# Final norm of a decoder step on one Trainium2 core: the factor table and three residuals are copied to PSUM and read there by VectorE

## The chip, the core and the metric

The kernel runs on one core of a Trainium2 chip. A core has five engines with a queue of instructions each: TensorE (PE in the profile, its weight loads PEld), VectorE (DVE), ScalarE (ACT), GpSimd (POOL) and SyncE (SP), which here only issues transfers. Tensors lie in the on-chip SBUF (128 partitions) or in the smaller PSUM, into which TensorE writes its products; VectorE and ScalarE reach both. The metric is the device time of one execution in microseconds (us), the median over several runs.

## What is computed

The reference is one step of a decoder layer: attention and a gated recurrence, then a mixture of experts, each between two RMS norms. 512 prompt rows and 8 sample rows of 1024 numbers pass through it. The change touches only the last line of the layer:

```
ffn = hier_moe(h, ...)
x = x + gt_f * rms_norm(ffn, g_post_ffn[l])

def rms_norm(x, g):
    y = xf * lax.rsqrt(jnp.mean(xf * xf, axis=-1, keepdims=True) + NORM_EPS)
    return (y * g).astype(x.dtype)
```

In words: each row of the experts' sum is multiplied by a factor per column (gate times norm weight), then by one number per row (the reciprocal root mean square), and the residual `x` is added.

## The kernel before

Everything up to the end of the experts stays as it was. Each expert's last step scatters 96 rows, adding them into the DRAM tensor `Y` (indirect transfer of GpSimd, line 1669). The last of them is issued in `finish(len(units) - 1, ...)`. Ahead of it the residuals are loaded into tiles of the ring of weight buffers, which is free by then: `at_end[t]` for t = 0 to 3 (128 rows each) and 4 (the 8 sample rows), and `GF`, the factors of the prompt's columns repeated on 128 partitions, is loaded into a sixth such tile. All of these are SBUF tiles; in the trace they go by the ring's names (`x`, `ewr`). After a branch that is taken only if an expert overflowed, the pool `fp` is opened and `srow` loads `gfs`, the 8 sample rows' own factors (tile `row`, issued on ScalarE's queue, line 1305).

Then comes the final norm, a loop over t in the order 4, 0, 1, 2, 3:

- SyncE loads 128 rows (8 for t = 4) of `Y` into a tile `y` (line 1837).
- ScalarE squares the row and sums it up into `ssf` (line 1841), and takes the square root (line 147).
- The product with the factors, `yg` (line 1842), is on VectorE for t in `ONDVE` = (0, 3) and on GpSimd for 4, 1 and 2.
- VectorE takes the reciprocal of `ssf` (line 148).
- VectorE's `scalar_tensor_tensor` (line 1846) computes `yg` * `ssf` + residual into `y`; for t = 3 in two halves.
- SyncE writes `y` out (line 1847).

The order of each queue at this place is made by a scheduler, so it isn't quite the order of the code. Each engine takes its own queue in order and waits for what an instruction needs. All elements are 32-bit floats.

Of the kernel before, what the change touches and what calls it, by code (L numbers as in the profile page):

```python
# [11 lines left out]
F32 = mybir.dt.float32  # L12
# [4 lines left out]
AF = mybir.ActivationFunctionType  # L17
ALU = mybir.AluOpType
AX = mybir.AxisListType
PSUM = bass.MemoryType.PSUM  # L20
DRAM = bass.MemoryType.DRAM

D = 1024
# [9 lines left out]
REUSE = "tile"  # L33
# [10 lines left out]
ONDVE = (0, 3)  # L44
# [20 lines left out]
def body(tc, I, O):  # L65
    nc = tc.nc
    es = ExitStack()
    dve, act, pool, pe, sp = nc.vector, nc.scalar, nc.gpsimd, nc.tensor, nc.sync
# [4 lines left out]
    def open_pool(name, bufs, stack, side="left"):  # L73
        return stack.enter_context(tc.tile_pool(name=name, bufs=bufs, side=side, reuse_waits=REUSE))

    psum = []
# [31 lines left out]
    def v2(t):  # L108
        return t.rearrange("p (h n) -> p h n", h=2)
# [35 lines left out]
    def rstd(ss):  # L145

        act.activation(ss, ss, AF.Sqrt, scale=1.0 / D, bias=epst[0:ss.shape[0]])
        dve.reciprocal(ss, ss)  # L148
        return ss
# [1081 lines left out]
    for t in range(5):  # L1231
        n = 128 if t < 4 else 8
# [70 lines left out]
    def srow(pl, g, j, **kw):  # L1303
        row = pl.tile([8, 2, 512], F32, name="row", **kw)
        act.dma_start(row, m4[g, j, :, 0:8, :].rearrange("q r n -> r q n"))
        return row
# [434 lines left out]
    with tc.manual_schedule(engines=MANUAL and {getattr(nc, e).engine for e in MANUAL}):  # L1741
# [5 lines left out]
        for o in ORD_M:  # L1747
            u = k[o] if o in k else 0
            if o in k:
                k[o] += 1  # L1750
                w, c = units[min(u, len(units) - 1)]
# [63 lines left out]
    at_end = [ring[c](F32) for c in ends]  # L1815
    spare = [x for c, x in enumerate(ring) if c not in ends]
    for t in range(5):
        n = 128 if t < 4 else 8
        sp.dma_start(at_end[t][0:n], X1[t, 0:n])
    GF = v2(at_end[5])  # L1820
# [6 lines left out]
    s_w.close()  # L1827


    fp = open_pool("fp", 2, es)  # L1830
    gfs = srow(fp, 1, 1, bufs=1)
    tc.keep_in_program_order(act.preload_act_table_set("sqrt_and_others"))
    ys = []
    for t in (4, 0, 1, 2, 3):
        n = 128 if t < 4 else 8
        y = fp.tile([128, D], F32, name="y", bufs=5)[:n]
        sp.dma_start(y, Y[128 * t:128 * t + n])
        jk = fp.tile([128, D], F32, name="jk")[:n]
        yg = fp.tile([128, D], F32, name="yg", bufs=3)[:n]
        ss = fp.tile([128, 1], F32, name="ssf", bufs=5)[:n]  # L1840
        act.activation(jk, y, AF.Square, accum_out=ss)
        (dve if t in ONDVE else pool).tensor_tensor(v2(yg), v2(y), GF if t < 4 else gfs, op=ALU.mult)  # L1842
        r = rstd(ss)
        out_ = O["yp"][t] if t < 4 else O["ys"]
        for c in (slice(0, 512), slice(512, D)) if t == 3 else (slice(0, D),):
            dve.scalar_tensor_tensor(y[:, c], yg[:, c], r, at_end[t][0:n, c], op0=ALU.mult, op1=ALU.add)  # L1846
            sp.dma_start(out_[:, c], y[:, c])
    es.close()

# [132 lines left out]
```

## Time and profile before

| | |
|---|---|
| median of 3 runs | 790.48 us (789.93 to 792.44) |
| the profiled execution's own time | 791.27 us |
| its span, first to last instruction | 789.6 us |
| busy: TensorE, VectorE, ScalarE, GpSimd | 83%, 59%, 47%, 23% of the span |
| the last `Y` scatter issued by GpSimd | at 761.79 us of the span |
| loads of `y` issued | from 768.35 us |
| last operation of VectorE ends | at 785.67 us |

Busy shares are means over the whole span. The final norm is the last stretch of it, from about 768 us on; TensorE has nothing to do there, and only the instructions of the other four count. Times of the trace are counted from the start of the span, in microseconds; the profiled execution's own time is 1.7 us above its span.

### The profile page before, as it was taken

What the parts mean: (1) busy time and instruction counts of PE and PEld (TensorE: products, weight loads), DVE (VectorE), ACT (ScalarE), POOL (GpSimd) and SP (SyncE); (2) the same over time, 40 slices, a digit from 0 to 9 for tenths busy, and PEclk for the clock granted to TensorE, in tenths of its full rate; (3) what the DMA queues carried; (4) which work ended last, traced back from release to release, by engine and by line L of the source; (5) the groups of instructions that cost most, each with busy time, mean ns of one, the idle gap of its engine ahead of it and who ended that gap; (6) DMA issues with size and microseconds to landing.
All of it is one profiled execution on the core that took longest, in us unless ns stands there. A gap on an engine that the chain in (4) does not pass through costs nothing. (4 is left out here: it accounts for less than half of the span.)

```text
span 789.6 us, 13169 instructions
## 1 busy us (share of the span) xinstructions
PE 651.7 (83%) x4495; PEld 490.3 (62%) x4495; DVE 464.0 (59%) x1140; ACT 374.1 (47%) x759; POOL 183.3 (23%) x208
## 2 busy tenths in 40 slices
PE   3885988998999999897999739995288899999930
PEld 1663866687878788885676426564255577666620
DVE  4523613345867765577643544356865976888806
ACT  4212512334455547623444234445445766888723
POOL 1000310002130131425432112435301223222114
PEclk9898999999999999999999958997588999999975
DMA  8876798866454632106221485338698889998515
GB/s 302 262 256 218 258 315 295 316 197 205 141 175 130 182 118 73 56 4 262 94 81 55 102 303 177 112 123 319 212 358 295 263 222 287 359 333 296 148 29 213
DMA packets 74604, 160.81 MB, mean 204 GB/s; under 512 B 11346, under 2 KB 39538, under 8 KB 74146
## 3 DMA queue, kind: packets, MB, share of 16 engines
q1 hardware_dynamic: 59844, 125.98, 46.6%
q10 hardware_dynamic: 10654, 25.39, 9.9%
q0 software_dynamic: 4032, 8.53, 5.1%
q8 instruction: 37, 0.61, 0.3%
q14 instruction: 37, 0.30, 0.1%
HBM read 145.29 MB, written 24.28 MB: 215 GB/s over the span
## 5 line engine op out<-in xcount | busy, mean ns | idle before, releaser
L563 PE MATMUL pp<-hhi,wh 128*128 128x260 f32 x256 | 75.6, 295 | 0.3 <-ACT kvt L441 0.3
L563 PE MATMUL pp<-hlo,wh 128*128 128x260 f32 x256 | 74.4, 291 | 0.0
L563 PE MATMUL pp<-hhi,wl 128*128 128x260 f32 x256 | 74.2, 290 | 0.0
L1669 POOL DMA_INDIRECT Y<-ot,gi x17 | 24.4, 1438 | 130.1 <-ACT ot L1668 123.0
L563 PEld LDWEIGHTS pp<-hhi,wh 128*128 128x128 f32 x256 | 49.4, 193 | 2.7 <-issue 2.0
L563 PEld LDWEIGHTS pp<-hhi,wl 128*128 128x128 f32 x256 | 49.3, 193 | 2.4 <-issue 2.3
L563 PEld LDWEIGHTS pp<-hlo,wh 128*128 128x128 f32 x256 | 49.4, 193 | 1.4 <-issue 1.2
L655 ACT ACTIVATE jn<-P,M 128x128 bf16<-128x128 f32 (+3 forms) x64 | 35.9, 560 | 27.3 <-DVE M L653 21.8
L113 DVE TENSOR_TENSOR wl<-wr,wh 128x1024 fp32r<-128x1024 f32 x9 | 11.2, 1250 | 39.8 <-ACT wh L112 39.8
L1058 ACT ACTIVATE PT<-mm 128x256 f32<-128x256 f32 x80 | 23.9, 388 | 19.8 <-PE mm L1054 19.7
L1640 PE MATMUL pf<-ewi,xh 128*96 128x512 f32 x72 | 30.2, 419 | 2.0 <-ACT xh L112 2.0
L653 DVE CUSTOM_DVE_ANT_0 P<-mm,tb 128x128 f32<-128x128 f32 (+3 forms) x64 | 29.0, 483 | 4.0 <-PE mm L646 3.9
L397 PE MATMUL mm<-hhi,wh 128*128 128x260 f32 x144 | 29.9, 288 | 1.3 <-ACT wh L112 1.3
L1640 PE MATMUL pf<-ewi,xl 128*96 128x512 f32 x72 | 29.5, 409 | 1.2 <-DVE xl L113 1.2
L112 ACT ACTIVATE wh<-wr 128x1024 fp32r<-128x1024 f32 x9 | 9.5, 1057 | 43.3 <-DMA wr<-in_wi 25.9
L397 PE MATMUL mm<-hlo,wh 128*128 128x260 f32 x144 | 30.0, 285 | 0.0
L397 PE MATMUL mm<-hhi,wl 128*128 128x260 f32 x144 | 29.7, 287 | 0.0
L646 PE MATMUL mm<-ka,qs 128*128 128x512 f32 (+2 forms) x112 | 27.6, 354 | 0.1
L1054 PE MATMUL mm<-qs,ka 128*128 128x512 f32 x80 | 26.6, 405 | 0.0
L1667 ACT ACTIVATE ot<-mm 96x512 f32<-96x512 f32 x17 | 10.1, 594 | 33.3 <-PE mm L1664 33.3
L397 PEld LDWEIGHTS mm<-hhi,wh 128*128 128x128 f32 x144 | 22.2, 188 | 5.0 <-issue 3.4
L299 PEld LDWEIGHTS po<-cg,w1c 128*128 128x128 f32 x160 | 21.5, 214 | 5.7 <-issue 3.3
(651 smaller groups left out, 1885.1 us busy)
## 6 DMA issues: line engine op xcount, KB each, us to landing
ewr<-in_ew SPq DMA_DIRECT2D x37, 512.0 KB
wa<-in_wa SPq DMA_DIRECT2D x16, 1024.0 KB
wr<-in_wi ACTq DMA_DIRECT2D x25, 512.0 KB
ewt<-in_ew SPq DMA_DIRECT2D x24, 512.0 KB
cg<-in_cc SPq DMA_DIRECT2D x64, 128.0 KB
ewh<-in_ew SPq DMA_DIRECT2D x16, 512.0 KB
x<-in_ew SPq DMA_DIRECT2D x15, 512.0 KB
mh<-in_wa SPq DMA_DIRECT2D x13, 512.0 KB
```

The lines of the kernel that those rows point to most:

```text
L113: (eng or dve).tensor_tensor(lo, src, hi.bitcast(F32), op=ALU.subtract)
L299: pe.matmul(p[:, 128 * k:128 * k + 128], w1c[:, k, s, :], cg[:, :, k, s, :], start=(s == 0), stop=(s == 7))
L397: pe.matmul(p[:, hf, 0:260], a[:, k, :], b[:, k, hf * 260:hf * 260 + 260], start=(k == 0 and j == 0), stop=(k == KT - 1 and j == 2))
L563: pe.matmul(p[:, 0:260], a[:, k, :], b[:, k, c], start=(k == 0 and j == 0), stop=(k == KT - 1 and j == 2))
L646: pe.matmul(o, QS[g][:, h % 4, qc], KA[g][:, j, a:b], start=(j == 0), stop=(j == 1))
L653: dve.tensor_tensor_reduce(out=p, in0=sb[:, br], in1=tb0[:, 384 - 128 * i:512].rearrange("p (k n) -> p k n", n=128), scale=SL[h], scalar=1 ...
L655: act.activation(jn[:, 0:128 * (i + 1)], p.rearrange("p k n -> p (k n)"), AF.Exp, scale=-1.0, bias=M[:, 0, i, br, h:h + 1], accum_out=M[:, ...
L1054: pe.matmul(S[:, br], KS[g][:, q, br, j], QS[g][:, :, qc], start=False, stop=(q == 1))
L1058: act.activation(PT[:, :, h], S4[:, :, h], AF.Exp, scale=-SL[4 * g + h])
L1640: pe.matmul(pg, a[:, k, :], b[:, wk_], start=(k == 0 and j == 0), stop=(k == 7 and j == 2))
L1667: act.activation(o3[:, 0], pd[:, 0], AF.Copy)
L1669: pool.indirect_dma_start(out=Y, out_offset=bass.IndirectOffsetOnAxis(ap=gix, axis=0), in_=ot, in_offset=None, bounds_check=T - 1, oob_is_ ...
```

## The change

Two copies of what VectorE reads are put into PSUM before the loop: `GFP`, a copy of `GF` (by VectorE), and `xp0`, `xp1`, `xp4`, copies of the residuals 0 (by VectorE), 1 and 4 (by ScalarE). The PSUM pool of the experts is closed first, and a new one, `fpp`, is opened for the four tiles. VectorE's products of t = 0 and 3 read `GFP`; its `scalar_tensor_tensor` of t = 4, 0 and 1 read the PSUM copies. GpSimd's products still read `GF` in SBUF, and the residuals of t = 2 and 3 stay in SBUF. The loop is cut into three, loads, products and sums, so that all loads are written first; `yg` has 5 buffers instead of 3 and `jk` 1 instead of 2.

```
+    psum.pop(0)[0].close()
+    fpp = es.enter_context(tc.tile_pool(name="fpp", bufs=1, space=PSUM, reuse_waits=REUSE))
     fp = open_pool("fp", 2, es)
+
+    GFP = fpp.tile([128, 2, 512], F32, name="GFP")
+    dve.tensor_copy(GFP, GF)
+    beside = {}
+    for t in (4, 0, 1):
+        n = 128 if t < 4 else 8
+        beside[t] = fpp.tile([128, D], F32, name=f"xp{t}")[0:n]
+        if t:
+            act.activation(beside[t], at_end[t][0:n], AF.Copy)
+        else:
+            dve.tensor_copy(beside[t], at_end[t])
     gfs = srow(fp, 1, 1, bufs=1)
     tc.keep_in_program_order(act.preload_act_table_set("sqrt_and_others"))
     ys = []
+    rows_, r_ = {}, {}
     for t in (4, 0, 1, 2, 3):
         n = 128 if t < 4 else 8
         y = fp.tile([128, D], F32, name="y", bufs=5)[:n]
         sp.dma_start(y, Y[128 * t:128 * t + n])
-        jk = fp.tile([128, D], F32, name="jk")[:n]
-        yg = fp.tile([128, D], F32, name="yg", bufs=3)[:n]
+        rows_[t] = y, fp.tile([128, D], F32, name="yg", bufs=5)[:n]
+    for t in (4, 0, 1, 2, 3):
+        y, yg = rows_[t]
+        n = y.shape[0]
+        jk = fp.tile([128, D], F32, name="jk", bufs=1)[:n]
         ss = fp.tile([128, 1], F32, name="ssf", bufs=5)[:n]
         act.activation(jk, y, AF.Square, accum_out=ss)
-        (dve if t in ONDVE else pool).tensor_tensor(v2(yg), v2(y), GF if t < 4 else gfs, op=ALU.mult)
-        r = rstd(ss)
+        (dve if t in ONDVE else pool).tensor_tensor(v2(yg), v2(y), gfs if t == 4 else GFP if t in ONDVE else GF, op=ALU.mult)
+        r_[t] = rstd(ss)
+    for t in (4, 0, 1, 2, 3):
+        y, yg = rows_[t]
+        n = y.shape[0]
         out_ = O["yp"][t] if t < 4 else O["ys"]
         for c in (slice(0, 512), slice(512, D)) if t == 3 else (slice(0, D),):
-            dve.scalar_tensor_tensor(y[:, c], yg[:, c], r, at_end[t][0:n, c], op0=ALU.mult, op1=ALU.add)
+            dve.scalar_tensor_tensor(y[:, c], yg[:, c], r_[t], beside.get(t, at_end[t][0:n])[:, c], op0=ALU.mult, op1=ALU.add)
             sp.dma_start(out_[:, c], y[:, c])
```

How VectorE's queue changes behind the branch, in one piece of the difference. `x_8103` is `GF`, `ewr_8098` the residual 0, `x_8099` to `x_8102` the residuals 1 to 4; `xp_9627`, `xp_9629`, `xp_9625` are `xp0`, `xp1`, `xp4`:

```order
+L1835 COPY GFP<-x_8103 128x1024
+L1843 COPY xp_9627<-ewr_8098 128x1024
+L1859 TENSOR_TENSOR yg<-y,GFP 128x1024
 L148 RECIPROCAL ssf<-ssf 8x1
-L1842 TENSOR_TENSOR yg<-y,x_8103 128x1024
-L1846 SCALAR_TENSOR_TENSOR y<-yg,ssf,x_8102 8x1024
+L1866 SCALAR_TENSOR_TENSOR y<-yg,ssf,xp_9625 8x1024
 L148 RECIPROCAL ssf<-ssf 128x1
-L1846 SCALAR_TENSOR_TENSOR y<-yg,ssf,ewr_8098 128x1024
+L1866 SCALAR_TENSOR_TENSOR y<-yg,ssf,xp_9627 128x1024
 L148 RECIPROCAL ssf<-ssf 128x1
-L1846 SCALAR_TENSOR_TENSOR y<-yg,ssf,x_8099 128x1024
```

Two copies stand in front; the first product moves ahead of the first reciprocal. Behind these rows the queue goes on with the sum of t = 1, as the next rows show:

```order
+L1866 SCALAR_TENSOR_TENSOR y<-yg,ssf,xp_9629 128x1024
 L148 RECIPROCAL ssf<-ssf 128x1
-L1842 TENSOR_TENSOR yg<-y,x_8103 128x1024
-L1846 SCALAR_TENSOR_TENSOR y<-yg,ssf,x_8100 128x1024
+L1859 TENSOR_TENSOR yg<-y,GFP 128x1024
 L148 RECIPROCAL ssf<-ssf 128x1
-L1846 SCALAR_TENSOR_TENSOR y<-yg,ssf,x_8101 128x512 x2
+L1866 SCALAR_TENSOR_TENSOR y<-yg,ssf,x_8100 128x1024
+L1866 SCALAR_TENSOR_TENSOR y<-yg,ssf,x_8101 128x512 x2
```

The last reciprocal moves ahead of the sum of t = 2. On ScalarE, behind the same branch, the two copies come ahead of the load of `row`:

```order
+L1841 ACTIVATE xp_9625<-x_8102 8x1024
+L1841 ACTIVATE xp_9629<-x_8099 128x1024
 L1305 DMA row<-MOD 8x2x512
-L1832 ACT_TABLE_LOAD
-L1841 ACTIVATE jk,ssf<-y 8x1024
+L1845 ACT_TABLE_LOAD
+L1858 ACTIVATE jk,ssf<-y 8x1024
```

The load of `row` and the loading of the square root's table move back by two copies. GpSimd's three products and SyncE's loads and writes keep their order.

## Rows read from the trace of the kernel before

**Rows 1.** Chain that ended last, first and fifth of its 6 pieces: start, us, what

```profile
781.84 1.12 DVE yg L1842
...
784.26 0.75 DVE y L1846
```

**Rows 2.** Waits of SyncE's queue from 740 us on: us in total, times, longest

```profile
SPq L1837 <- DMA Y<-ewt,gi: 21.7, 1, 21.7
...
SPq L1971 <- DMA out_yp<-y: 1.9, 1, 1.9
```

**Rows 3.** Timeline of VectorE in the final norm: start, duration, instruction [idle before <- releaser]

```profile
772.78 1.22 DVE L1842 TENSOR_TENSOR yg<-y,x 128x1024 f32<-128x1024 f32 x1 [0.81 <-DMA y<-Y]
...
773.92 1.27 DVE L1846 SCALAR_TENSOR_TENSOR y<-yg,ssf,x 8x1024 f32<-8x1024 f32 x1
...
775.12 0.14 DVE L148 RECIPROCAL ssf<-ssf 128x1 f32<-128x1 f32 x1
...
775.30 3.18 DVE L1846 SCALAR_TENSOR_TENSOR y<-yg,ssf,ewr 128x1024 f32<-128x1024 f32 x1
...
778.65 3.11 DVE L1846 SCALAR_TENSOR_TENSOR y<-yg,ssf,x 128x1024 f32<-128x1024 f32 x1
...
781.76 1.20 DVE L1842 TENSOR_TENSOR yg<-y,x 128x1024 f32<-128x1024 f32 x1
...
782.88 1.27 DVE L1846 SCALAR_TENSOR_TENSOR y<-yg,ssf,x 128x1024 f32<-128x1024 f32 x1
...
784.26 1.41 DVE L1846 SCALAR_TENSOR_TENSOR y<-yg,ssf,x 128x512 f32<-128x512 f32 x2
```

**Rows 4.** Timeline of GpSimd: its last scatter and the three products

```profile
761.79 1.40 POOL L1669 DMA_INDIRECT Y<-ewt,gi  x1 [4.72 <-DMA Y<-ot,gi]
...
770.35 2.33 POOL L1842 TENSOR_TENSOR yg<-y,row 8x1024 f32<-8x1024 f32 x1 [7.16 <-DMA y<-Y]
...
774.14 3.27 POOL L1842 TENSOR_TENSOR yg<-y,x 128x1024 f32<-128x1024 f32 x1 [1.45 <-DMA y<-Y]
...
777.36 3.32 POOL L1842 TENSOR_TENSOR yg<-y,x 128x1024 f32<-128x1024 f32 x1
```

**Rows 5.** Timeline near 505 us, VectorE and GpSimd, every input in SBUF

```profile
504.86 2.30 DVE L1377 SCALAR_TENSOR_TENSOR mg<-tg,ssa,tab 128x1024 f32<-128x1024 f32 x1 [0.52 <-POOL tg L1372]
...
504.79 1.28 POOL L1363 TENSOR_TENSOR mg<-x,row 8x512 f32<-8x512 f32 x1
```

**Rows 6.** Timeline near 360 and 390 us; pt and pf are PSUM tiles

```profile
360.42 0.68 DVE L992 TENSOR_TENSOR AT<-pt,triu 128x512 f32<-128x512 f32 x1
...
359.35 2.32 POOL L1102 TENSOR_TENSOR S<-S,hsn 128x1024 f32<-128x1024 f32 x1 [0.53 <-DMA S<-in_s]
...
389.84 1.11 DVE L1000 SCALAR_TENSOR_TENSOR S<-S,sx,pf 128x128 f32<-128x128 f32 x3
...
389.86 0.83 POOL L978 TENSOR_TENSOR qj<-qj,sx 128x384 f32<-128x384 f32 x1
```

**Rows 7.** Groups by line and shape: xcount | busy us, mean ns | idle before

```profile
L1372 POOL TENSOR_TENSOR tg<-x,tab 128x1024 f32<-128x1024 f32 x4 | 9.6, 2390 | 11.6 <-DVE x L1369 7.4 <-issue 2.8 <-DVE ssa L1364 1.4
...
L555 DVE CAST wh<-wr 128x1024 fp32r<-128x1024 f32 x16 | 11.1, 691 | 11.7 <-PE pp L563 7.3 <-DMA wr<-in_wi 3.0 <-PE mm L397 1.4
...
L1000 DVE SCALAR_TENSOR_TENSOR S<-S,sx,pf 128x128 f32<-128x128 f32 x12 | 4.1, 345 | 0.3
```

**Rows 8.** Timeline of ScalarE behind the branch and at its last row

```profile
762.51 0.51 ACTq L1305 DMA_DIRECT2D row<-MOD  x1
763.06 1.28 ACT L1832 ACT_TABLE_LOAD   x1 [3.28 <-ACTq L1824]
...
777.18 1.04 ACT L1841 ACTIVATE jk<-y 128x1024 f32<-128x1024 f32 x1
...
778.35 0.29 ACT L147 ACTIVATE ssf<-ssf,epst 128x1 f32<-128x1 f32 x1
```

**Rows 9.** Windows, one stretch: length; busy PE, PEld, DVE, ACT, POOL; PEclk, DMA share, GB/s

```profile
772.00:774.00 2.00, 0.00 (x0) 0.00 (x0) 1.22 (x2) 1.20 (x3) 0.69 (x1) 0.50 1.03 389
```

## The prediction

> **What bounds the kernel now.** I read the chain of waits first. Its six pieces, from 781.84 us on, lie on VectorE and its queue but for 0.02 us [rows 1], so the final norm's VectorE queue sets the end. SyncE's waits show what stands on either side of it: the loads of `y` wait for the last scatter into `Y`, and at the very end SyncE waits 1.9 us for the last write [rows 2]. The scatter and the write don't change; between them lies the stretch that the change touches.
>
> Then the timeline of VectorE [rows 3]. The reader is to see two durations that don't fit. The sum (`scalar_tensor_tensor`) of 1024 columns takes 1.27 us for t = 4 and for t = 2, but 3.18 for t = 0 and 3.11 for t = 1, same operation, same shape of 1024 columns. Put GpSimd's timeline beside it [rows 4]: its products of 128x1024 take 3.27 and 3.32 us, while four like them elsewhere took 2.39 each [rows 7]. The ends fit a hold in turns. GpSimd's first product starts at 774.14, inside VectorE's sum of t = 4 (773.92 to 775.19); 775.19 + 2.33 = 777.52 against its real end, 774.14 + 3.27 = 777.41. VectorE's sum of t = 0 is issued at 775.30 and ends at 778.48, which is 1.07 behind that end. GpSimd's second product, issued at 777.36, ends at 780.68, 2.20 behind 778.48. VectorE's sum of t = 1 ends at 781.76, 1.08 behind 780.68. So each op waits until the other engine's op is over, then needs about its own length. These four have two tensor inputs in SBUF on both engines. It isn't peculiar to this place: near 505 us a sum of 1024 columns takes 2.30 us, and the GpSimd product beside it ends at 506.07, 1.09 before the sum's end at 507.16 [rows 5].
>
> Does an op with one input in PSUM wait too? Two places answer [rows 6]. A VectorE product of 512 columns with one input in PSUM runs 360.42 to 361.10, wholly inside a GpSimd product (359.35 to 361.67), in 0.68 us. Three sums with exactly the operands that the change makes (tensor in SBUF, a number per row, tensor in PSUM) take 1.11 us together next to a GpSimd product that lies within the same microsecond and takes 0.83; 1.11 / 3 = 0.37, starts and ends overlapping, against a mean of 0.345 over all twelve [rows 7]. Neither is held.
>
> **The change part by part.** *The holds.* The sums of t = 4, 0 and 1, and the product of t = 3, get one input in PSUM, so neither engine should hold the other. I lay VectorE's new queue out with steps from one start to the next, as [rows 3] have them without a hold: product to next 773.92 - 772.78 = 1.14; sum to reciprocal 775.12 - 773.92 = 1.20; reciprocal to next 775.30 - 775.12 = 0.18. The first product starts at 772.78 as now, since it waits for a load. In the new order: product 0 at 772.78; reciprocal 773.92; sum 4 at 774.10; reciprocal 775.30; sum 0 at 775.48; reciprocal 776.68; sum 1 at 776.86; reciprocal 778.06; product 3 at 778.24; reciprocal 779.38; sum 2 at 779.56; the two halves of sum 3 from 780.76, over 1.41 later at 782.17. Now it is 784.26 + 1.41 = 785.67. The gain is 3.50 us. As a check from the other side: the two long sums lose 3.18 - 1.27 = 1.91 and 3.11 - 1.27 = 1.84, together 3.75; the rest is the reciprocal of t = 4, which now stands behind product 0 (it was hidden in a wait), and my cautious step behind it.
>
> *What the new queue waits for.* GpSimd's product 1 starts at 774.14 (a load releases it) and should take 2.39, to 776.53; sum 1 wants it at 776.86. Product 2 then ends at 778.92; sum 2 wants it at 779.56. Both are in time, by 0.33 and 0.64. ScalarE's last root is done at 778.35 + 0.29 = 778.64 [rows 8], and its reciprocal stands at 779.38; of the five it has the least to spare. The last `y` is there by 777.18, when it is squared.
>
> *The copies.* They aren't in the trace. On VectorE two of 128x1024: at least 0.69 (a cast of this size, SBUF to SBUF) [rows 7], at most about a product's 1.22 [rows 3]. I take 1.22, since PSUM is not SBUF and the longer one is the safer; 2.44 in all. The cover is the idle stretch before 772.78: VectorE waits there for `y`, as ScalarE does until the loads come, and what the copies read was loaded before. Without this cover they would cost 1.4 to 2.4. On ScalarE two copies of some 1.05 us each (a square of this size took 1.04, [rows 8]) go ahead of the load of `row`, which moves from 762.51 to about 764.6, and the table from 763.06 to 765.2, over at 766.5. GpSimd needs `row` at 770.35. Loads of `y` issued from about 768.35 on release that instruction within 2.0 us, so a load of the same size issued at 764.6 is there by about 766.6. Cost: nothing.
>
> *PSUM as a source.* From SBUF, a sum of 512 columns takes 0.75 us [rows 1] and one of 1024 takes 1.27 [rows 3]: 0.52 for 512 columns, 0.13 for 128, so 128 columns would be 0.75 - 3 x 0.13 = 0.36. With an input in PSUM they took 0.345 [rows 7]: no dearer; I take zero. At the other end, were the whole 0.37 - 0.345 = 0.03 of [rows 6] its price, five ops would cost 0.13. [...]
>
> *The writes.* Each is 512 KB; at the 389 GB/s of the loads [rows 9] that is 1.35 us, and the sums come at steps of 1.4 to 2.7, so the writes don't pile up more than now. The tail behind the last sum (785.67 to 789.6) stays; I allow 0.4 for it.
>
> Sum: profiled execution 791.27 - 3.50 = 787.8. It stands 0.8 above the median, 790.48, within the runs' spread; from the median, 790.48 - 3.50 = **787.0 us**.
>
> **The rivals.**
>
> *The hold stays.* VectorE still reads `yg` from SBUF in every sum and GpSimd still reads `y` and `GF` there; if the hold comes from any SBUF reading, the change does nothing: 790.5, or 0.2 more for the reciprocal. Against it speak [rows 6], though with ops shorter than these. 8%.
>
> *GpSimd was slow by itself.* If its 3.27 and 3.32 are its own pace here, product 2 ends at 780.68 again; sum 2 starts at 780.7, the halves at 781.9, the end is 783.3: 2.35 gained, 788.1. The 2.39 of [rows 7] speaks against it; that loads run at the same time is for it. 6%.
>
> *The copies hold up the last scatter.* GpSimd prepares it for 1.40 us at 761.79 [rows 4], VectorE is idle then and could be copying. Were GpSimd held for both copies whole, everything behind it, loads included, would come 2.44 later: 790.48 - 3.50 + 2.44 = 789.4; held for part of one, some 788. [...] 5%.
>
> *Slower: reading PSUM is dear at this size.* Five ops on the path (products 0 and 3, sums 4, 0, 1) now read 1024 columns from two PSUM banks; no row has that. At 3.50 / 5 = 0.7 us more for each the gain is gone; slower by over 0.3% it gets from (3.50 + 2.4) / 5 = 1.2 more for each, which is each at twice its length: 792.9 or more. No row of 512 columns shows a trace of it. 4%.
>
> **How the numbers follow.** The forecast has the remaining 77%, and with the bounds above 786.4 to 787.7; runs scattered from 789.93 to 792.44, so that I go down to 785.6 and up to 789.0, which takes in GpSimd's own slowness and a short hold of the scatter. About 0.3%, 2.4 us, is what a measurement of this kernel can tell from no change: faster is below 788.1. Faster: 76 of the 77, half of the 6 and 1 of the 5 make 80%; same: 8 + 3 + 4 + 1 = 16%; slower 4%.
>
> **What the profile after would show.** Right: both VectorE sums of t = 0 and 1 at 1.2 to 1.4 us while GpSimd's products run; those at 2.3 to 2.5 each, with no gap between them; VectorE's last op over some 20.4 us behind the last scatter's issue (782.17 - 761.79), now 23.9; copies over by about 767; `row` there before `y`. Wrong: sums still at 3.1 (hold stays); sums short and sum 2 waiting for GpSimd (its own pace); loads of `y` issued later than 6.6 us behind the scatter (768.35 - 761.79; the copies' doing); products and sums with PSUM inputs well over 1.3 (PSUM is dear). It would also be wrong if the writes, coming earlier and closer, made the tail longer than its 3.9 us.

## The result and the profile after

The change takes 788.83 us in the median of 20 runs, the kernel before 792.34 us in 20 runs beside it: ratio 0.9937, 95% interval 0.9913 to 0.9961. That is 0.63% of 792.34 or 5.0 us faster (3.1 to 6.9); the medians lie 3.5 us apart. The ratio counts only the runs within 1.5% of the fastest of their kernel, 14 of 20 with the change and all 20 before, so it flatters the change; the medians over all runs give 0.9956. The profiled execution took 785.33 us with a span of 783.6.

The timeline of the kernel after, all engines together (start, duration, instruction; `xp` and `GFP` are the PSUM copies; lines 1851 to 1867 are 1837 to 1847 of before):

```profile
759.48 1.40 POOL L1669 DMA_INDIRECT Y<-ewt,gi  x1 [4.86 <-DMA Y<-ot,gi]
760.05 1.23 DVE L1835 COPY GFP<-x 128x1024 f32<-128x1024 f32 x1 [6.51 <-ACTq L1824]
760.17 1.02 ACT L1841 ACTIVATE xp<-x 8x1024 f32<-8x1024 f32 x1 [2.81 <-ACTq L1824]
760.28 0.52 ACTq L1305 DMA_DIRECT2D row<-MOD  x1
761.13 1.00 ACT L1841 ACTIVATE xp<-x 128x1024 f32<-128x1024 f32 x1
761.19 1.22 DVE L1843 COPY xp<-ewr 128x1024 f32<-128x1024 f32 x1
762.15 1.28 ACT L1845 ACT_TABLE_LOAD   x1
766.08 2.31 SPq L1851 DMA_DIRECT2D y<-Y  x5
768.01 2.33 POOL L1859 TENSOR_TENSOR yg<-y,row 8x1024 f32<-8x1024 f32 x1 [7.13 <-DMA y<-Y]
...
770.17 1.22 DVE L1859 TENSOR_TENSOR yg<-y,GFP 128x1024 f32<-128x1024 f32 x1 [7.76 <-DMA y<-Y]
...
771.30 0.14 DVE L148 RECIPROCAL ssf<-ssf 8x1 f32<-8x1 f32 x1
...
771.52 4.67 POOL L1859 TENSOR_TENSOR yg<-y,x 128x1024 f32<-128x1024 f32 x2 [1.18 <-DMA y<-Y]
771.66 1.27 DVE L1866 SCALAR_TENSOR_TENSOR y<-yg,ssf,xp 8x1024 f32<-8x1024 f32 x1 [0.21 <-DVE ssf L148]
...
773.03 1.28 DVE L1866 SCALAR_TENSOR_TENSOR y<-yg,ssf,xp 128x1024 f32<-128x1024 f32 x1
...
774.48 1.28 DVE L1866 SCALAR_TENSOR_TENSOR y<-yg,ssf,xp 128x1024 f32<-128x1024 f32 x1
...
775.75 1.20 DVE L1859 TENSOR_TENSOR yg<-y,GFP 128x1024 f32<-128x1024 f32 x1
...
776.94 2.59 DVE L1866 SCALAR_TENSOR_TENSOR y<-yg,ssf,x 128x1024 f32<-128x1024 f32 x3
```

The sums of t = 0 and 1, which took 3.18 and 3.11 us [rows 3], take 1.28 each, while GpSimd's two products run beside them; and these take 4.67 together, 2.33 each, where they took 3.27 and 3.32 [rows 4]. VectorE waits nowhere for more than 0.21 us between 770.17 and 779.53. From the start of its first product to the end of its last sum it needs 779.53 - 770.17 = 9.36 us; before it was 785.67 - 772.78 = 12.89.

Of the chain that ended last (start, us, what), the last three of nine pieces, and of SyncE's waits (us in total, times, longest) the two that stand on either side:

```profile
777.02 1.18 DVE y L1866
778.21 0.66 DVEq L1991
778.87 0.66 DVE y L1866
```

```profile
SPq L1851 <- DMA Y<-ewt,gi: 22.3, 1, 22.3
...
SPq L1991 <- DMA out_yp<-y: 2.1, 1, 2.1
```

The end still hangs on VectorE's queue, and the stretch still lies between the last scatter and the last write, as in [rows 1, 2].

Not all of the 6.0 us between the two spans belongs to the change. The last scatter, ahead of everything that was edited, is issued at 759.48 us instead of 761.79. Both kernels were therefore profiled again (e8 and e9 below); only what lies behind the last scatter, where TensorE has no work left, is compared:

| profiled execution | last scatter issued | from there to VectorE's last op | from there to the end of the span |
|---|---|---|---|
| before | 761.79 | 23.88 | 27.81 |
| before again (e9) | 758.18 | 23.87 | 27.72 |
| the change | 759.48 | 20.05 | 24.12 |
| the change again (e8) | 770.08 | 19.97 | 24.02 |

The place of the scatter moves by more than the change is worth, either way for either kernel. What follows it repeats within 0.1 us: the change is worth 27.81 - 24.12 = 3.69 and 27.72 - 24.02 = 3.70 us. That the two agree so closely is chance. In the first pair VectorE's work, from first product to last sum, is 3.53 us shorter, its first product starts 0.30 earlier behind the scatter, and what follows its last op is 0.14 longer; in the second pair these are 3.87, 0.03 and 0.20. This also says how the ratios are to be read: e9, the kernel before against itself, came out at 0.996 (0.993 to 0.999), so a measured ratio can be off by 0.4%, more than its interval admits. By the times alone a gain of 3.7 us in 792, 0.5%, can hardly be told from that. The experiments were judged by the last stretch of their profiles first.

### The profile page after: what moved, and what is told of

It is laid out like the page before. It is cut to its first block, busy times and chain, and to the rows that moved or that the text cites. A ratio compares the mean times of both kernels' runs of the same rounds, so it can differ in the third digit from the quotient of the medians.

```text
span 783.6 us, 13171 instructions
## 1 busy us (share of the span) xinstructions
PE 651.9 (83%) x4495; PEld 490.6 (63%) x4495; DVE 461.7 (59%) x1142; ACT 376.0 (48%) x761; POOL 181.1 (23%) x208
## 3 DMA queue, kind: packets, MB, share of 16 engines
q0 software_dynamic: 4032, 8.53, 4.9%
## 5 line engine op out<-in xcount | busy, mean ns | idle before, releaser
L1615 POOL DMA_INDIRECT XG<-H,gi x18 | 19.4, 1079 | 26.6 <-PE pt L1628 12.1
```

The costliest lines, as they stand in the source:

```text
L1615: pool.indirect_dma_start(out=xg, out_offset=None, in_=H2, in_offset=bass.IndirectOffsetOnAxis(ap=gix, axis=0), bounds_check=T - 1, oob_is ...
```

## The experiments

Theory: an op of VectorE and an op of GpSimd that both read two inputs from SBUF hold each other, one waiting till the other is over; an input in PSUM takes VectorE's op out of that. Rivals: the new order and buffers give the time; fresh tiles do, whatever the memory; the shared factor table is what is fought for; the long sums have another reason than GpSimd. The table names sums and products by their t: sum 4 is the `scalar_tensor_tensor` of t = 4, product 3 VectorE's second product. "Stretch" is VectorE's first product to last sum.

| | sum 4, 0, 1 (us) | product 3 | stretch | ratio to before, 95% interval |
|---|---|---|---|---|
| before | 1.27, 3.18, 3.11 | 1.20 | 12.89 | |
| the change | 1.27, 1.28, 1.28 | 1.20 | 9.36 | 0.9937 (0.9913 to 0.9961) |
| e1 order only | 1.27, 3.19, 3.12 | 1.20 | 12.76 | 1.0002 (0.9973 to 1.0030) |
| e2 PSUM, old order | 1.27, 1.28, 1.27 | 1.22 | 10.18 | 0.9957 (0.9924 to 0.9991) |
| e3 copies in SBUF | 3.20, 3.18, 1.28 | 1.20 | 13.23 | 0.9996 (0.9966 to 1.0027) |
| e4 residuals only | 1.27, 1.28, 1.28 | 1.92 | 10.08 | 0.9953 (0.9916 to 0.9990) |
| e5 factors only | 1.27, 3.18, 3.12 | 1.20 | 12.75 | 0.9968 (0.9929 to 1.0008) |
| e6 GpSimd writes only | 1.27, 1.29, 1.28 | 1.20 | 10.80 | one run |
| e7 all on VectorE | 1.27, 1.27, 1.27 | 1.19 | 11.49 | 0.9961 (0.9926 to 0.9995) |

**e1, the order alone.** In the changed kernel, without the copies:

```
-    GFP = fpp.tile([128, 2, 512], F32, name="GFP")
-    dve.tensor_copy(GFP, GF)
+    GFP = GF
...
-    for t in (4, 0, 1):
+    for t in ():
```

> The loop is cut in three and the buffers are those of the change, but nothing is copied: every VectorE op reads SBUF. VectorE's stretch here is the time from the start of its first product to the end of its last sum: 12.89 us before, 9.36 with the change. Theory (VectorE and GpSimd hold each other where both have two inputs in SBUF): the sums of t = 0 and 1 take 3.1 to 3.2 us again, GpSimd's two products 3.3 each, stretch 12.7 to 13.0 (13.7 if the sum of t = 4 is caught as well), ratio 0.997 to 1.003. Rival (the new order and buffers gave the time): sums at 1.27, stretch at most 9.6, ratio near 0.9955.

The timeline of e1 around the sums:

```profile
777.34 1.27 DVE L1863 SCALAR_TENSOR_TENSOR y<-yg,ssf,x 8x1024 f32<-8x1024 f32 x1
...
778.72 3.19 DVE L1863 SCALAR_TENSOR_TENSOR y<-yg,ssf,ewr 128x1024 f32<-128x1024 f32 x1
...
782.07 3.12 DVE L1863 SCALAR_TENSOR_TENSOR y<-yg,ssf,x 128x1024 f32<-128x1024 f32 x1
...
777.58 6.52 POOL L1856 TENSOR_TENSOR yg<-y,x 128x1024 f32<-128x1024 f32 x2 [1.44 <-DMA y<-Y]
```

All holds are back, on both engines. Order and buffers give 12.89 - 12.76 = 0.13 us.

**e2, the copies in the old loop.** The kernel before with the pool, the four copies and their readers put in, the loop left in one piece.

> The four copies to PSUM and their readers, but the loop in one piece and the buffers as before. Theory: sums of t = 4, 0 and 1 at 1.27 to 1.32, GpSimd's products at 2.3 to 2.4, stretch 9.2 to 10.2 (here the scheduler puts product 3 ahead of the sum of t = 1, behind a reciprocal that has to wait for ScalarE), ratio 0.995 to 0.997. Rival (order): stretch 12.9, ratio 1.

The timeline of e2:

```profile
775.87 1.22 DVE L1855 TENSOR_TENSOR yg<-y,GFP 128x1024 f32<-128x1024 f32 x1 [8.02 <-DMA y<-Y]
...
777.58 1.27 DVE L1859 SCALAR_TENSOR_TENSOR y<-yg,ssf,xp 8x1024 f32<-8x1024 f32 x1 [0.21 <-DVE ssf L148]
...
778.96 1.28 DVE L1859 SCALAR_TENSOR_TENSOR y<-yg,ssf,xp 128x1024 f32<-128x1024 f32 x1
780.65 0.35 DVE L148 RECIPROCAL ssf<-ssf 128x1 f32<-128x1 f32 x2 [0.41 <-ACT ssf L147]
...
777.66 4.68 POOL L1855 TENSOR_TENSOR yg<-y,x 128x1024 f32<-128x1024 f32 x2 [1.75 <-DMA y<-Y]
```

No op is held. The stretch is 0.8 longer than with the change. Half of that is a wait of 0.41 us for ScalarE's root, since here two reciprocals and product 3 stand ahead of the sum of t = 1; 0.2 more is lost at the start, where the sum of t = 4 begins 1.71 behind product 0 instead of 1.49. So the cut of the loop is worth something, but only once the holds are gone.

**e3, the copies in SBUF.** In the changed kernel:

```
-    psum.pop(0)[0].close()
-    fpp = es.enter_context(tc.tile_pool(name="fpp", bufs=1, space=PSUM, reuse_waits=REUSE))
+    fpp = open_pool("fpp", 1, es)
```

> The change word for word, but the pool of the four copies lies in SBUF. Theory: the holds are back, two or three of VectorE's sums at 2.3 to 3.3 us, stretch 12.7 to 13.8, ratio 0.997 to 1.004. Rival (fresh tiles, whatever memory): stretch 9.4. The copies SBUF to SBUF should take 0.69 us each on VectorE instead of 1.22. If such a copy keeps GpSimd from preparing its last scatter, that scatter takes up to 0.7 longer than its 1.40; if not, 1.40.

The timeline of e3: the last scatter with the first copy, ScalarE's second copy and the load of `row`, then products and sums:

```profile
762.46 1.40 POOL L1669 DMA_INDIRECT Y<-ewt,gi  x1 [5.19 <-ACTq L1824]
...
762.49 0.69 DVE L1834 COPY GFP<-x 128x1024 f32<-128x1024 f32 x1 [6.29 <-ACTq L1824]
...
769.18 1.06 ACT L1840 ACTIVATE xp<-x 128x1024 f32<-128x1024 f32 x1 [5.46 <-DMA Y<-ot,gi]
...
769.42 0.52 ACTq L1305 DMA_DIRECT2D row<-MOD  x1
...
775.51 3.20 DVE L1865 SCALAR_TENSOR_TENSOR y<-yg,ssf,xp 8x1024 f32<-8x1024 f32 x1
...
778.81 3.18 DVE L1865 SCALAR_TENSOR_TENSOR y<-yg,ssf,xp 128x1024 f32<-128x1024 f32 x1
...
782.15 1.28 DVE L1865 SCALAR_TENSOR_TENSOR y<-yg,ssf,xp 128x1024 f32<-128x1024 f32 x1
...
775.27 5.63 POOL L1858 TENSOR_TENSOR yg<-y,x 128x1024 f32<-128x1024 f32 x2 [1.02 <-issue]
```

The same copies in SBUF help nothing: it is the memory. Here the sum of t = 4 starts 0.24 behind GpSimd's first product and is caught, so GpSimd is through by the sum of t = 1. The first copy lies inside the preparing of the scatter, which takes its 1.40 all the same. One thing blurs this run: its second pair of copies waited for an earlier scatter to land (presumably because their tiles lie where its rows had been), so that `row` came late and GpSimd began later, 771.92 - 762.46 = 9.46 us behind the scatter's issue instead of 8.53.

**e4 and e5, one half each.** e4 copies only the residuals (`GFP = GF`), e5 only the factors (`for t in ():`).

> Only the residuals of t = 4, 0 and 1 are copied to PSUM; VectorE's two products read the factors in SBUF. Theory: the sums as with the change (1.27), the first product too (no GpSimd product beside it); product 3 meets the last 0.4 us of GpSimd's second product and takes 1.5 to 1.6 instead of 1.20; stretch 9.6 to 9.8, ratio 0.995 to 0.997. Rival (the factor table, read by both engines, is what they fight for): sums at 1.27 but product 3 held for a whole GpSimd product, or no gain: stretch 11 to 12.9.

> Only the factor table is copied to PSUM and read there by VectorE's two products; all residuals stay in SBUF. Theory: the sums of t = 0 and 1 (or 4 and 0, if the sum of t = 4 starts behind GpSimd's first product) take 3.1 to 3.3 us as before, stretch 12.7 to 13.8, ratio 0.997 to 1.004. Rival (the engines fight for the shared table): stretch 9.4, sums at 1.27.

The timeline of e4, product 3 and GpSimd's products:

```profile
773.76 1.92 DVE L1858 TENSOR_TENSOR yg<-y,x 128x1024 f32<-128x1024 f32 x1
...
769.92 4.67 POOL L1858 TENSOR_TENSOR yg<-y,x 128x1024 f32<-128x1024 f32 x2 [1.65 <-DMA y<-Y]
```

And of e5, the sums of t = 0 and 1:

```profile
777.22 3.18 DVE L1866 SCALAR_TENSOR_TENSOR y<-yg,ssf,ewr 128x1024 f32<-128x1024 f32 x1
...
780.57 3.12 DVE L1866 SCALAR_TENSOR_TENSOR y<-yg,ssf,x 128x1024 f32<-128x1024 f32 x1
```

The residuals carry most of the gain: 12.89 - 10.08 = 2.81 of 3.53 us. With them alone, product 3 meets GpSimd's second product, which ends at 774.59; product 3 ends 1.09 later, held for 0.7 us. I had expected 0.3 to 0.4, and a stretch of 9.6 to 9.8; GpSimd's products came 1.74 behind VectorE's first one here, 1.35 with the change, since a load came later. The factors alone give the queue nothing (12.75), and the engines don't fight for the table; but once the residuals are copied, the factors' copy is worth up to these 0.7 us. e5's ratio, 0.9968 with 1 inside its interval, would have left that open.

**e6, GpSimd busy but writing.** In the kernel before, for t = 1 and 2:

```
+        if t in (1, 2):
+            pool.tensor_tensor(yg[:, 0:8], y[:, 0:8], at_end[5][:, 0:8], op=ALU.mult)
+            for _ in range(3):
+                pool.memset(yg, 1.0)
```

> The kernel before, but GpSimd's products of t = 1 and 2 are cut to 8 columns and followed by three fills of the whole tile each, so GpSimd is busy and writes SBUF but hardly reads it; two of the five row blocks get ones instead of their products. Theory (the hold needs an SBUF-reading op on GpSimd): the sums of t = 0 and 1 take 1.27 us beside the fills, the fills 0.95 each. Rival (any GpSimd op on SBUF takes turns with a two-input VectorE op): at least one sum is 0.5 us longer, or a fill is stretched to 1.5 or more.

The timeline of e6:

```profile
777.59 0.98 POOL L1843 TENSOR_TENSOR yg<-y,x 128x8 f32<-128x8 f32 x1 [1.45 <-DMA y<-Y]
778.63 1.97 POOL L1845 MEMSET yg<- 128x1024 f32 x2
...
778.61 1.29 DVE L1851 SCALAR_TENSOR_TENSOR y<-yg,ssf,ewr 128x1024 f32<-128x1024 f32 x1
```

The sum of t = 0, all in SBUF, takes 1.29 us while GpSimd fills SBUF from 778.63 to 780.60. The two fills take 1.97 together, 0.98 each, where 0.95 was expected and the rival asked for 1.5; the sum of t = 1, also beside fills, takes 1.28. The product of 8 columns, which reads, takes 0.98 when it is issued into the sum of t = 4, and its twin 0.20 with nothing beside it. So in this run the fills, which only write, held no sum, and the product, which reads, was held.

**e7, no GpSimd beside the sums.** `ONDVE = (0, 1, 2, 3)` in the kernel before.

> The kernel before with one number changed: the products of t = 1 and 2 go from GpSimd to VectorE, everything stays in SBUF. Theory (two-input ops of both engines hold each other): with no GpSimd product beside them all of VectorE's sums take 1.27 and its four products 1.2; VectorE has two more products, 2.3 us, but loses holds of 3.75, so its stretch is 11.4 to 11.6 us against 12.89 before, and the kernel gains 1.4 us (ratio 0.998, not told from 1 by the times). Rival (the sums of t = 0 and 1 are slow for another reason, the loads or writes beside them): they stay at 3.1 and the stretch grows to about 15.

The timeline of e7:

```profile
769.21 2.34 POOL L1842 TENSOR_TENSOR yg<-y,row 8x1024 f32<-8x1024 f32 x1 [7.22 <-DMA y<-Y]
...
771.04 1.60 DVE L1842 TENSOR_TENSOR yg<-y,x 128x1024 f32<-128x1024 f32 x1 [0.20 <-DMA y<-Y]
...
774.95 1.27 DVE L1846 SCALAR_TENSOR_TENSOR y<-yg,ssf,ewr 128x1024 f32<-128x1024 f32 x1
...
777.34 1.27 DVE L1846 SCALAR_TENSOR_TENSOR y<-yg,ssf,x 128x1024 f32<-128x1024 f32 x1
```

The stretch is 11.49, inside the 11.4 to 11.6 that was worked out. VectorE does two products more and is done 1.4 us earlier: GpSimd's help had cost more than it gave. The first product shows a hold of its own, 1.60 instead of 1.22, by the end of GpSimd's product of 8 rows (771.55). That hold was not in the 11.4 to 11.6, so the good fit is partly luck. The time's ratio can't be told from that of e9, which ran beside it.

**e8 and e9, both kernels again.**

> The change once more. The issue of the last scatter marks what lies before the final norm; it came at 761.79 us before and 759.48 with the change. If that difference is only how fast the part before it happened to run, it falls anywhere between 757 and 766 here, as it did in the other profiles, and the time from it to VectorE's last op is 20.0 to 20.2 again; if the change makes the earlier part faster, it falls at 759 to 760 again, with the ratio near 0.993.

> The kernel before once more, for the same question: the last scatter anywhere between 757 and 766 us, and 23.7 to 24.0 from it to VectorE's last op, if the part before the final norm differs from run to run; at 761.5 to 762.5, if it is a trait of this kernel. Ratio 0.997 to 1.003.

The last scatter, the first product of VectorE, GpSimd's product beside it and the last sums, of e8 and then of e9:

```profile
770.08 1.40 POOL L1669 DMA_INDIRECT Y<-ewt,gi  x1 [4.37 <-DMA Y<-ot,gi]
...
778.84 2.34 POOL L1859 TENSOR_TENSOR yg<-y,row 8x1024 f32<-8x1024 f32 x1 [7.36 <-DMA y<-Y]
...
780.63 1.22 DVE L1859 TENSOR_TENSOR yg<-y,GFP 128x1024 f32<-128x1024 f32 x1 [7.15 <-DMA y<-Y]
...
787.44 2.61 DVE L1866 SCALAR_TENSOR_TENSOR y<-yg,ssf,x 128x1024 f32<-128x1024 f32 x3
```

```profile
758.18 1.40 POOL L1669 DMA_INDIRECT Y<-ewt,gi  x1 [4.55 <-DMA Y<-ot,gi]
...
766.96 2.33 POOL L1842 TENSOR_TENSOR yg<-y,row 8x1024 f32<-8x1024 f32 x1 [7.38 <-DMA y<-Y]
...
768.76 1.62 DVE L1842 TENSOR_TENSOR yg<-y,x 128x1024 f32<-128x1024 f32 x1 [0.17 <-DMA y<-Y]
...
780.63 1.42 DVE L1846 SCALAR_TENSOR_TENSOR y<-yg,ssf,x 128x512 f32<-128x512 f32 x2
```

The scatter came at 770.08 in e8, beyond the 757 to 766 that I had given, and at 758.18 in e9; the lengths behind it, 19.97 and 23.87, repeat. In e9 product 0 is held by GpSimd's product of 8 rows and takes 1.62; in e8 it reads the factors from PSUM, starts before the like product has ended (781.18) and takes 1.22. So the factors' copy is worth 0.4 us here too, when the first load comes early. e8 came out at 0.9916 (0.9870 to 0.9961) and e9 at 0.996, where 0.997 to 1.003 was expected, against the same runs of before; one over the other is 0.9956, 3.5 us of 792.

## Why the prediction was right, step by step

*The holds.* The step that carried the forecast held: 3.50 us was worked out, 12.89 - 9.36 = 3.53 measured, and e1, e2, e3, e6 and e7 leave none of the rivals named for the cause. The layout was near at every point; counted from the start of product 0, the sums of t = 4, 0, 1 and 2 were to start at 1.32, 2.70, 4.08 and 6.78, and started at 1.49, 2.86, 4.31 and 6.77; the end was to come at 9.39 and came at 9.36. Counted from the scatter's issue, VectorE's last op ended after 20.05 instead of 20.4, nearly all because product 0 started 0.30 earlier behind the scatter; the prediction has no term for that, and in e8 and e9 it is 0.03.

*The reciprocal behind product 0.* It cost more than its 0.18: the sum of t = 4 starts 0.36 behind it, 0.21 of it a wait for its result. So did the reciprocal ahead of the sum of t = 1, by 0.07. Two later steps (0.08 from a reciprocal to product 3, 0.07 from the last reciprocal to the sum of t = 2, instead of 0.18 each) gave that back: that the end fits within 0.03 us is errors cancelling.

*What the queue waits for.* GpSimd's products end at 776.19, 6.02 from product 0; the sum of t = 2 starts at 6.77. In time, as said, with 0.75 to spare against 0.64. ScalarE's last root is done at 776.37, 0.50 before its reciprocal, against 0.74. That GpSimd was slow by itself is refuted: 2.33 each.

*The copies.* 1.23 and 1.22 on VectorE, over at 762.41, long before 770.17; 1.02 and 1.00 on ScalarE. Free, as said. One detail was wrong: the load of `row` was not held back by two copies. It is issued 0.80 us behind the scatter's issue, 0.72 before [rows 4, 8], while ScalarE's first copy runs. In e3 the second copy had to wait for a transfer until 769.18, and the load was issued at 769.42: that wait held it back; the copies by themselves did not. Only the table moved, by 1.4.

*The copies holding up the scatter.* They lie beside its preparing (760.05 into 759.48 to 760.88) and it takes 1.40 or 1.41 in every profile, with copies or without. The loads of `y` start 766.08 - 759.48 = 6.60 behind its issue, 6.56 before; in e8 it is 6.79 and in e9 6.66. A sign of being wrong was any start later than 6.6, and e8 shows one, but by 0.2 us and not by the 2.44 of the two copies. In e3 a copy from SBUF to SBUF left the scatter at 1.40 as well, so no run shows GpSimd held by a copy there; from SBUF to SBUF that is one case.

*PSUM as a source.* 1.28 instead of 1.27 for a sum, 1.22 and 1.20 as before for a product: at most 0.01 for each op, and 0.02 for product 3 in e2. With the change that is at most 0.05 us for five ops, and the rival built on a high price falls. The upper bound of 787.7 fits 787.0 with 0.4 for the writes and 0.3 for PSUM; no run shows that 0.3, the runs showed the 0.05.

*The writes.* The tail behind the last sum is 783.6 - 779.53 = 4.07 us, 0.14 longer than 3.93; the allowance was 0.4.

*The time.* 787.0 was forecast from a median of 790.48; the medians came out at 788.83 and 792.34. The difference of the medians is the forecast's, the level is that of the runs: 788.83 lies just inside the stated 785.6 to 789.0, and above the 788.1 that I had called faster, since the kernel before came out 1.9 us above the 790.48 that I had started from. That the difference fits to 0.01 us is luck: what I had set down as the limit of the measurement, 2.4 us, was too small, as e9 came out 0.4%, 3.2 us, from the same kernel.

## What to carry to other kernels

Where VectorE and GpSimd work side by side, look for one op whose duration is about its own plus what is left of an op of the other engine: here the two held each other where both read two tensors and all of them lay in SBUF (sums of 3.18 and 3.11 us instead of 1.27, products of 3.27 and 3.32 instead of 2.33). Whether a GpSimd op with a single input does the same was not tried. One input of VectorE's op in PSUM ended it (sums of 1.28, products of 2.33), and the copies there were free, since they lay in a wait (over at 762.41, the first product at 770.17); such a copy was worth it for the inputs of ops that really ran beside GpSimd, here the residuals first (2.81 us), and the factors for 0.4 us (product 0 in e9) to 0.7 us (product 3 in e4). Judge an edit at the end of a kernel by the stretch from the last fixed event, not by the span, when the part ahead of it moves from run to run by more than the edit is worth.

## What was not expected of the hardware

A GpSimd op of 8 partitions held a VectorE op of 128 too (1.60 and 1.62 us instead of 1.22 in e7 and e9). A VectorE copy of 128x1024 floats took 0.69 us from SBUF to SBUF (e3) but 1.23 and 1.22 from SBUF to PSUM. And a transfer that stands behind two copies in ScalarE's queue was issued while the first of them ran (at 760.28, the copy from 760.17 to 761.19), but behind a wait of the second it was late (at 769.42 in e3).
